# Delta rule of a hybrid layer: four heads' key norms in one go, one decay matrix per head through DRAM, six jobs at a time, and two chunk chains half a head apart

## The chip, the cores and the metric

The kernel runs on 1 core of one Trainium2 chip. The metric is the device time of one execution in microseconds (us). The core has a matrix engine (PE, with its weight loads shown apart as PEld), a vector engine (DVE), an activation engine (ACT), a general engine (POOL), and a queue engine (SP) that issues most of the DMA transfers. Each engine works through its own instructions in program order.

## The reference, cut to what matters

Two layers act on x (512 tokens, 2048 channels). The even layer is chunked attention plus an mLSTM; nothing of it changes. The odd layer projects to 6160 columns, runs an RG-LRU on eight blocks and a gated delta rule on eight heads, and projects back. The delta rule is what changes:

```python
    decay = jnp.cumsum(gc, axis=-1)
    gam = jnp.exp(jnp.where(tril, decay[..., :, None] - decay[..., None, :], NEG))
    kbeta = kc * bc[..., None]
    a_mat = jnp.where(strict, jnp.einsum('nbhtd,nbhsd->nbhts', kbeta, kc) * gam, 0.0)
    t_inv = lax.linalg.triangular_solve(eye + a_mat, ...)
    ...
    def step(st, inp):
        un, wn, qdn, qkn, kdn, dln = inp
        v_new = un - jnp.einsum('bhtk,bhkv->bhtv', wn, st)
        o = jnp.einsum('bhtk,bhkv->bhtv', qdn, st) + jnp.einsum('bhts,bhsv->bhtv', qkn, v_new)
        st = dln[..., None, None] * st + jnp.einsum('bhsk,bhsv->bhkv', kdn, v_new)
        return st, o
```

q and k are normalised to unit length first. The kernel uses chunks of 128 tokens, so a head has four of them.

## The kernel before

**Stream and jobs.** `run` walks over a list of units: four K-tiles of one weight tile each. A unit of the odd layer's input projection is 12 matmuls of 128x512 (lines 291 to 293: high half by high half, high by low, low by high of float32 values split in two). The weights of a unit come by DMA on SP, are split by an ACT copy (line 247) and a DVE subtraction (line 248), and this split is issued `AHEAD` = 5 units before the unit's matmuls. After every second K-tile, that is after six matmuls, `run` calls `tick`, and `tick` lets each active job (a Python generator) issue its next piece of instructions:

```python
    def tick(self):
        while len(self.active) < self.nact and self.jobs:
            self.active.append(self.jobs.popleft())
        for g in list(self.active):
            if next(g, self) is self:
                self.active.remove(g)
```

`yield from self.wait("name")` lets `LAG["name"]` ticks pass. So the order on every engine is fixed when the program is built; a LAG that is too short shows as a matmul in PE's queue whose input isn't there yet, and the weight stream waits behind it.

**The odd layer.** The stream brings the eight heads' k tiles, then x and gate tiles of LRU blocks 0 to 3, then q, v, z of heads 0 to 7, then LRU blocks 4 to 7 (48 weight tiles), and then the output projection, which reads the 16 tiles of `y1` (LRU 0 to 3, heads 0 to 7, LRU 4 to 7); its first four weight tiles run interleaved, four K-tiles of each in turn. The jobs stand in this order: `start1` (norm and gates), eight `delta_keys`, `solve`, four `lru_block`, then `inverse(h+1)` and `delta_head(h)` in turn, and four `lru_block`. Four jobs are active at a time until `solve` is done, and six from then on.

- `delta_keys(h)` (lines 1155 to 1196): convolution, SiLU, four transposes (1165), squares and their sum (1173); writes k and its transpose to DRAM (1162, 1174); then the inverse norm by 14 vector instructions on 128x4 values (1179, helper lines 623 to 629) and the columns derived from it (1181 to 1186); the decay matrix with the strict triangle by two POOL subtractions and one Exp (`gamma`, lines 1149 to 1152), times a column on POOL (1188); k by k on PE (1193); product on DVE (1194), written to DRAM as `ud`.
- `solve` (1198 to 1224): inverts the 32x32 diagonal blocks of all heads at once, 31 steps of one DVE product (1214) and one DVE sum (1220), both growing with n*n, each step followed by a wait of `1 + n * n // LAG['sv.n']` ticks.
- `inverse(h)` puts the blocks together to 128x128 inverses; it starts when `solve` is done and `self.heads >= h - 1`, and scales the transposed keys on POOL (1241).
- `delta_head(h)`: convolutions of q and v; the decay matrix a second time, now with the diagonal (POOL 1278, 1279, Exp 1282, times a column on POOL 1284); q by k (1291), transposes of v (1297); then, once the head before has finished (`while self.heads < h`), the chain over four chunks: state by keys (`dh.ks`, 1310, into DVE 1313), inverse by that (`dh.xr`, 1316, into DVE 1318), update of the state (`dh.kv`, 1322, into DVE 1325 or 1327). The output matmuls (1311, 1329) go between these steps. Then norm, gate and `put`.

Weight tiles' results are evicted by DVE with the row norms (`evict`, line 453; `evict_pad`, line 481). Scratch tiles come from small pools: `tmp` (6 buffers), `ev` (13), `act` slots (37), and 4 PSUM banks `pm` for the jobs.

Of the kernel before, what the change touches and what calls it, by code (L numbers as in the profile page):

```python
# [8 lines left out]
F32 = mybir.dt.float32  # L9
F32R = mybir.dt.float32r  # L10
# [6 lines left out]
P = 128  # L17
# [19 lines left out]
EPS = 1e-6  # L37
NEG = -1e30
# [10 lines left out]
Y1_ORDER = list(range(4)) + [8 + i for i in range(8)] + list(range(4, 8))  # L49
# [3 lines left out]
for _h in range(4):  # L53
# [15 lines left out]
    "conv": 2, "gam": 8, "sv": 8,  # L69
    "sv.n": 300,  # L70
# [5 lines left out]
    "dh.kq": 5, "dh.vt": 1, "dh.first": 4, "dh.ks": 1, "dh.xr": 2, "dh.kv": 2, "dh.ss": 4,  # L76
# [4 lines left out]
class Net:  # L81
# [9 lines left out]
    def __init__(self, ctx, tc, a):  # L91
# [32 lines left out]
        self.heads = self.turn = 0  # L124
# [608 lines left out]
    def start0(self, raw):  # L733
# [20 lines left out]
        self.tri1 = self.triangle(-NEG, -1)  # L754
# [260 lines left out]
    def layer1(self):  # L1015
# [4 lines left out]
        self.ud = self.dr.tile([8, P, S], F32, name="ud")  # L1020
        self.xd = self.dr.tile([P, 32, 32], F32, name="xd")
# [5 lines left out]
        for n in range(4):  # L1027
            add((n, "x"), self.evict_pad)
            add((n, "zc"), self.evict)
        for h in range(8):  # L1030
            add((h, "q"), self.evict_pad)
            add((h, "v"), self.evict_pad)
            add((h, "z"), self.evict)
        for n in range(4, 8):
            add((n, "x"), self.evict_pad)
            add((n, "zc"), self.evict)
# [3 lines left out]
        self.jobs += [self.delta_keys(h) for h in range(8)]  # L1040
        self.jobs += [self.solve()]
        self.jobs += [self.lru_block(n) for n in range(4)]
        self.jobs += [self.inverse(0)]
        for h in range(8):
            self.jobs += [self.inverse(h + 1)] if h < 7 else []
            self.jobs += [self.delta_head(h)]
        self.jobs += [self.lru_block(n) for n in range(4, 8)]
# [5 lines left out]
    def start1(self):  # L1053
# [8 lines left out]
        self.kcols = self.mp.tile([P, 8, 4, 4], F32, name="kcols")  # L1062
# [28 lines left out]
    def delta_gates(self, g):  # L1091
# [35 lines left out]
        nc.vector.tensor_scalar(self.ncols, self.cols[:, 1], -1.0, None, ALU.mult)  # L1127
        self.t["gates1"] = True
# [16 lines left out]
    def gamma(self, h, db, g, tri):  # L1145

        nc = self.nc
        yield
        nc.gpsimd.tensor_tensor(self.c4(g), self.c4(db), self.mask_bc(tri), ALU.subtract)
        nc.gpsimd.tensor_tensor(self.c4(g), self.c4(g), self.col_bc(self.cols[:, 0, :, h]), ALU.subtract)  # L1150
        yield from self.wait("gam")
        nc.scalar.activation(g, g, AF.Exp)
        yield

    def delta_keys(self, h):
# [10 lines left out]
        kt, g = self.ev(), self.ev()  # L1166
        sq = self.tmp()
        nc.scalar.activation(kt, ps, AF.Copy)
        ss = self.small(P, 4)
        nc.scalar.activation(sq, kt, AF.Square)  # L1170
        db = self.dec_bc(h)
        yield from self.wait(2)
        nc.vector.tensor_reduce(ss, self.c4(sq), AX.X, ALU.add)
        nc.gpsimd.dma_start(self.ktd[h], kt)
        while "gates1" not in self.t:
            yield

        nc.vector.tensor_scalar(ss, ss, 4 * EPS, None, ALU.add)
        r = self.rsqrt_cols(ss)
        kc = self.kcols[:, h]  # L1180
        nc.vector.tensor_copy(kc[:, 0], r)
        nc.vector.scalar_tensor_tensor(kc[:, 1], ss, 0.5, r, ALU.mult, ALU.mult)
        nc.vector.tensor_tensor(kc[:, 2], r, self.cols[:, 3, :, h], ALU.mult)
        nc.vector.tensor_tensor(kc[:, 3], r, self.cols[:, 2, :, h], ALU.mult)
        nb = self.small(P, 4)
        nc.vector.scalar_tensor_tensor(nb, kc[:, 2], -1.0, r, ALU.mult, ALU.mult)
        yield from self.gamma(h, db, g, self.tri1)
        nc.gpsimd.tensor_tensor(self.c4(g), self.c4(g), self.col_bc(nb), ALU.mult)
# [5 lines left out]
        nc.vector.tensor_tensor(g, g, ps, ALU.mult)  # L1194
        nc.gpsimd.dma_start(self.ud[h], g)
# [30 lines left out]
    def inverse(self, h):  # L1226

        nc = self.nc
        while "solved" not in self.t or self.heads < h - 1:
            yield  # L1230
# [10 lines left out]
        nc.gpsimd.tensor_tensor(self.c4(kd), self.c4(kd), self.col_bc(self.kcols[:, h, 3]), ALU.mult)  # L1241
# [24 lines left out]
    def delta_head(self, h):  # L1266
        nc, mp = self.nc, self.mp
        cs = lambda t, c: t[:, c * P : c * P + P]
        while self.heads < h - 1:
            yield  # L1270
# [4 lines left out]
        kc = self.kcols[:, h]  # L1275
# [5 lines left out]
        yield from self.wait("gam")  # L1281
# [17 lines left out]
        nc.vector.tensor_tensor(self.c4(vt), self.c4(ps), self.col_bc(kc[:, 1]), ALU.mult)  # L1299
# [4 lines left out]
        op = self.psum("dh.o")  # L1304
        st = None
        for c in range(4):
            rt = cs(vt, c)
# [187 lines left out]
```

## Time and profile before

| | |
|---|---|
| runs | 1854.64, 1988.14, 1854.49 us; median 1854.64 |
| profiled execution | 1853.82 us, its span 1852.0 us |
| busy PE / DVE / ACT / POOL | 1829.2 / 1340.3 / 877.9 / 217.5 us |
| mean granted TensorE clock | 0.998 |

The page gives busy time by engine, the span in 40 slices, the DMA queues, the chain that ended last, and groups of instructions. A busy PE isn't PE at its peak, since matmuls are pipelined and overlap: a row's duration is longer than the distance to the next one. So the distances between matmuls are read in the timeline, and the waits of PE in the view of waits. The layer that changes lies between about 1030 and 1720 us.

### The profile page before, as it was taken

How to read it: one execution, taken by the hardware profiler on the slowest of the kernel's cores; microseconds unless marked ns; L12 is line 12 of the kernel's file. 1: busy time of each engine (PE TensorE's matmuls, PEld its weight loads, DVE VectorE, ACT ScalarE, POOL GpSimd, SP SyncE). 2: the span in 40 equal slices, each digit the busy share in tenths (PEclk: the TensorE clock that was granted, in tenths of full speed). 3: DMA queues.
4: the chain of work that ended last, by engine and by line, in shares of the span. 5: the costliest groups of instructions: out<-in, count | busy, mean ns of one | idle time of the engine just before them, and what ended most of it. 6: DMA issues, size and time to landing. Idle time of an engine off the chain costs nothing.

```text
span 1852.0 us, 27588 instructions
## 1 busy us (share of the span) xinstructions
PE 1829.2 (99%) x10162; PEld 1566.2 (85%) x10162; DVE 1340.3 (72%) x2367; ACT 877.9 (47%) x1528; POOL 217.5 (12%) x262
## 2 busy tenths in 40 slices
PE   9999999999999999999999999999999999999999
PEld 7789899989889899988899788887788878787998
DVE  6768658798647368787766799889647667768664
ACT  6365445655435354665434553454333434566332
POOL 0010101110100101011111023301202122000000
PEclk9999999999999999999999999999999999999999
DMA  6243333333434343237554444433433433245542
GB/s 226 80 136 103 108 115 113 110 100 116 127 98 121 101 124 102 88 97 221 187 160 147 126 142 155 150 114 104 143 103 109 118 114 100 77 134 161 176 135 73
DMA packets 137288, 232.13 MB, mean 125 GB/s; under 512 B 22896, under 2 KB 32240, under 8 KB 137152
## 3 DMA queue, kind: packets, MB, share of 16 engines
q1 hardware_dynamic: 129488, 208.60, 37.0%
q0 software_dynamic: 5360, 17.57, 2.6%
q10 hardware_dynamic: 2304, 4.20, 0.6%
q8 instruction: 80, 1.31, 0.3%
q14 instruction: 56, 0.46, 0.1%
HBM read 203.79 MB, written 26.51 MB: 124 GB/s over the span
## 4 chain that ended last, share of the span: by engine, by line
PE 80%; DVE 12%; issue 3%; ACT 2%; DMA 2%; SPq 1%; DVEq 0%; ACTq 0%
PE pp L365 39%; PE pp L291 8%; PE pp L293 8%; PE pp L292 8%; PE pp L427 3%; PE pp L429 3%; PE pp L428 3%; DVE act L248 3%; DVE act L1214 1%; DMA act<-in_xT 1%; ACT act L247 1%; DVE act L1137 1%; DVE ev L1137 1%; DMA wr<-in_wi 0%; SPq L1207 0%
## 5 line engine op out<-in xcount | busy, mean ns | idle before, releaser
L365 PE MATMUL pp<-act,act 128*128 128x256 f32 (+1 forms) x4884 | 794.5, 322 | 0.0
L365 PEld LDWEIGHTS pp<-act,act 128*128 128x128 f32 x4884 | 707.0, 190 | 70.1
L248 DVE TENSOR_TENSOR act<-wr,act 128x512 fp32r<-128x512 f32 x719 | 507.7, 721 | 242.1 <-ACT act L247 239.6
L247 ACT ACTIVATE act<-wr 128x512 fp32r<-128x512 f32 x719 | 419.9, 622 | 188.6 <-DVE wr L222 61.0
L291 PE MATMUL pp<-act,act 128*128 128x512 f32 x960 | 389.4, 406 | 2.0 <-ACT act L563 1.3
L293 PE MATMUL pp<-act,act 128*128 128x512 f32 x960 | 377.0, 393 | 3.8 <-DVE act L248 3.7
L292 PE MATMUL pp<-act,act 128*128 128x512 f32 x960 | 376.0, 392 | 0.9 <-DVE act L564 0.8
L293 PEld LDWEIGHTS pp<-act,act 128*128 128x128 f32 x960 | 180.9, 188 | 45.0 <-DVE act L248 6.0
L291 PEld LDWEIGHTS pp<-act,act 128*128 128x128 f32 x960 | 181.5, 189 | 41.5 <-issue 3.8
L292 PEld LDWEIGHTS pp<-act,act 128*128 128x128 f32 x960 | 181.4, 189 | 36.5 <-DVE act L564 1.5
L427 PE MATMUL pp<-act,act 128*128 128x512 f32 x256 | 100.3, 392 | 0.0
L429 PE MATMUL pp<-act,act 128*128 128x512 f32 x256 | 99.7, 390 | 0.0
L428 PE MATMUL pp<-act,act 128*128 128x512 f32 x256 | 99.7, 389 | 0.0
L222 DVE TENSOR_TENSOR wr<-wr,wr 128x512 f32<-128x512 f32 x111 | 77.1, 695 | 1.3
L381 ACT ACTIVATE ee<-pp 128x512 f32<-128x512 f32 x74 | 44.1, 595 | 61.6 <-PE pp L365 61.3
L980 POOL TENSOR_SCALAR pq<-pq,mx 128x512 f32<-128x512 f32 (+3 forms) x32 | 47.3, 1491 | 188.7 <-DVE mx L977 188.7
L528 POOL DMA_DIRECT2D yd<-ev x20 | 11.4, 570 | 401.5 <-DVE ev L1011 163.9
L429 PEld LDWEIGHTS pp<-act,act 128*128 128x128 f32 x256 | 48.1, 188 | 10.1
L428 PEld LDWEIGHTS pp<-act,act 128*128 128x128 f32 x256 | 48.1, 188 | 9.7
L427 PEld LDWEIGHTS pp<-act,act 128*128 128x128 f32 x256 | 48.1, 188 | 9.6
L784 DVE TENSOR_TENSOR ev<-ev,pp 128x512 f32<-128x512 f32 x32 | 22.0, 688 | 46.9 <-PE pp L365 43.2
L593 ACT ACTIVATE act<-ev 128x512 fp32r<-128x512 f32 x40 | 25.0, 629 | 52.2 <-DVE ev L938 31.0
(334 smaller groups left out, 1992.0 us busy)
## 6 DMA issues: line engine op xcount, KB each, us to landing
wr<-in_wi SPq DMA_DIRECT2D x216, 256.0 KB
wr<-in_ws SPq DMA_DIRECT2D x100, 256.0 KB
wr<-in_wd SPq DMA_DIRECT2D x100, 256.0 KB
wr<-in_wv SPq DMA_DIRECT2D x64, 256.0 KB
wr<-in_wso SPq DMA_DIRECT2D x48, 256.0 KB
wr<-in_wdo SPq DMA_DIRECT2D x48, 256.0 KB
wr<-in_wo SPq DMA_DIRECT2D x32, 256.0 KB
ev<-x1d SPq DMA_DIRECT2D x28, 256.0 KB
```

Source lines behind the costliest of these rows:

```text
L222: sub = lambda o, x, y: nc.vector.tensor_tensor(o, x, y, ALU.subtract)
L247: nc.scalar.activation(h, w, AF.Copy)
L248: nc.vector.tensor_tensor(l, w, h.bitcast(F32), ALU.subtract)
L291: nc.tensor.matmul(ps, h[:, j, :], xh, start=k == 0, stop=False)
L292: nc.tensor.matmul(ps, h[:, j, :], xl, start=False, stop=False)
L293: nc.tensor.matmul(ps, l[:, j, :], xh, start=False, stop=k == KT - 1)
L365: mm = lambda o, x, y, start=False: nc.tensor.matmul(o, x, y, start=start, stop=True, skip_group_check=True)
L381: nc.scalar.activation(e, ps, AF.Copy)
L427: nc.tensor.matmul(ps, xh, h, start=k == 0, stop=False)
L428: nc.tensor.matmul(ps, xh, l, start=False, stop=False)
L429: nc.tensor.matmul(ps, xl, h, start=False, stop=k == KT - 1)
L980: nc.gpsimd.tensor_scalar(rows(b), rows(b), mx[:, 3, b : b + 1], None, ALU.mult)
```

## The change

- `delta_keys` is cut in three. `keys(h)` goes as far as the sum of squares. `key_norms(h0)` computes the norms of four heads at once, on 128x16 values. `couplings(h)` reads k back from DRAM, builds the decay matrix once (with the diagonal) by one POOL subtraction and four Exps with the decay as a bias column, writes it to DRAM (`gd`), and multiplies k by k with it and with a column in four DVE instructions.
- `delta_head` reads `gd` instead of building the decay matrix; norms no longer scale it, and the column of `vn` takes their square instead. `inverse` scales the transposed keys by four ACT copies instead of one POOL product.
- The heads' turn is counted in chunks (`self.blocks`): a head's chain starts when the chain before it has done two of four chunks, and `inverse` and `delta_head` start half a head earlier too. The steps' waits are longer (`dh.ks` 1 to 2 ticks, `dh.xr` 2 to 3, `dh.kv` 2 to 3). The seven output matmuls of a head stand together at its end.
- Six jobs are active from the start of the layer, and `solve` waits longer (`sv.n` 300 to 220). `lru_block` takes its gate weights' buffers from the common pools. The order of the stream is the same, written in another way.

```diff
+RS = 12
-    "conv": 2, "gam": 8, "sv": 8,
-    "sv.n": 300,
+    "conv": 2, "gam": 5, "dk.db": 3, "dh.q": 6, "sv": 8,
+    "sv.n": 220,
-    "dh.kq": 5, "dh.vt": 1, "dh.first": 4, "dh.ks": 1, "dh.xr": 2, "dh.kv": 2, "dh.ss": 4,
+    "dh.kq": 5, "dh.vt": 1, "dh.first": 4, "dh.ks": 2, "dh.xr": 3, "dh.kv": 3, "dh.ss": 4,
...
-        self.jobs += [self.delta_keys(h) for h in range(8)]
+        self.jobs += [self.keys(h) for h in range(4)] + [self.key_norms(0)]
+        self.jobs += [f(h + 4 * i) for h in range(4) for i, f in ((1, self.keys), (0, self.couplings))]
+        self.jobs += [self.key_norms(4)] + [self.couplings(h) for h in range(4, 8)]
         self.jobs += [self.solve()]
...
-        self.nact = 4
+        self.nact = 6
...
+    def key_norms(self, h0):
+
+        nc = self.nc
+        yield from self.take(*((h, "ss") for h in range(h0, h0 + 4)))
+        while "gates1" not in self.t:
+            yield
+        half, b, nb = [self.kcols[:, i, h0 : h0 + 4] for i in range(3)]
+        flat = half.rearrange("p h c -> p (h c)")
+        nc.vector.tensor_scalar(flat, flat, 4 * EPS, None, ALU.add)
+        r = self.rsqrt_cols(flat).rearrange("p (h c) -> p h c", c=4)
+        nc.vector.tensor_tensor(b, r, r, ALU.mult)
+        nc.vector.scalar_tensor_tensor(half, half, 0.5, r, ALU.mult, ALU.mult)
+        nc.vector.tensor_tensor(b, b, self.cols[:, 3, :, h0 : h0 + 4].rearrange("p c h -> p h c"), ALU.mult)
+        nc.vector.tensor_scalar(nb, b, -1.0, None, ALU.mult)
+        for h in range(h0, h0 + 4):
+            self.t[h, "norms"] = True
+
+    def couplings(self, h):
+
+        nc = self.nc
+        yield from self.take((h, "norms"))
+        db, k, g = self.dec_bc(h), self.ev(), self.ev()
+        nc.sync.dma_start(k, self.kfd[h])
+        yield from self.wait("dk.db")
+        nc.gpsimd.tensor_tensor(self.c4(db), self.c4(db), self.mask_bc(self.tri), ALU.subtract)
+        yield from self.wait("gam")
+        for c in range(4):
+            nc.scalar.activation(self.c4(g)[:, c], self.c4(db)[:, c], AF.Exp, bias=self.ndec[:, c, h : h + 1])
+        nc.gpsimd.dma_start(self.gd[h], g)
+        yield from self.wait("dk.kk")
+        ps = self.psum("dk.kk")
+        u = db
         for c in range(4):
             kc = k[:, c * P : c * P + P]
             nc.tensor.matmul(ps[:, c * P : c * P + P], kc, kc, start=True, stop=True)
+        for c in range(4):
+            nc.vector.scalar_tensor_tensor(self.c4(u)[:, c], self.c4(ps)[:, c], self.kcols[:, 2, h, c : c + 1], self.c4(g)[:, c], ALU.mult, ALU.mult)
+        nc.gpsimd.dma_start(self.ud[h], u)
...
     def inverse(self, h):
-        while "solved" not in self.t or self.heads < h - 1:
+        while "solved" not in self.t or self.blocks < 4 * h - 6:
...
-        nc.gpsimd.tensor_tensor(self.c4(kd), self.c4(kd), self.col_bc(self.kcols[:, h, 3]), ALU.mult)
+        for c in range(4):
+            nc.scalar.activation(self.c4(kd)[:, c], self.c4(kd)[:, c], AF.Copy, scale=self.cols[:, 2, c, h : h + 1])
...
     def delta_head(self, h):
-        while self.heads < h - 1:
+        while self.blocks < 4 * h - 6:
...
+        nc.sync.dma_start(att, self.gd[h])
-        nc.gpsimd.tensor_tensor(self.c4(att), self.c4(db), self.mask_bc(self.tri), ALU.subtract)
-        nc.gpsimd.tensor_tensor(self.c4(att), self.c4(att), self.col_bc(self.cols[:, 0, :, h]), ALU.subtract)
-        yield from self.wait("gam")
-        nc.scalar.activation(att, att, AF.Exp)
+        yield from self.wait("dh.q")
-        nc.gpsimd.tensor_tensor(self.c4(att), self.c4(att), self.col_bc(kc[:, 0]), ALU.mult)
...
-        while self.heads < h:
+        while self.blocks < 4 * h - 2:
...
-                nc.tensor.matmul(cs(op, c), st, cs(q, c), start=True, stop=False)
...
-            nc.tensor.matmul(cs(op, c), vn, cs(att, c), start=not c, stop=True)
...
+        op = self.psum("dh.o")
+        for c in range(4):
+            if c:
+                nc.tensor.matmul(cs(op, c), st[c], cs(q, c), start=True, stop=False)
+            nc.tensor.matmul(cs(op, c), vn[c], cs(att, c), start=not c, stop=True)
```

## Rows read from the trace of the kernel before

**Rows 1.** The page: span, and PE's busy time and share.
```profile
span 1852.0 us, 27588 instructions
...
PE 1829.2 (99%) x10162; PEld 1566.2 (85%) x10162; DVE 1340.3 (72%) x2367; ACT 877.9 (47%) x1528; POOL 217.5 (12%) x262
```

**Rows 2.** Timeline of PE, first and last of 43 matmuls: start, us, what.
```profile
1126.37 0.40 PE L292 MATMUL pp<-act,act 128*128 128x512 f32 x1
...
1135.90 0.39 PE L292 MATMUL pp<-act,act 128*128 128x512 f32 x1
```

**Rows 3.** Waits of PE, 1030 to 1740 us: us in total, times, longest.
```profile
PE pp L293 <- DVE act L248: 3.7, 2, 2.2
PE dh_vt L1297 <- DVE act L672: 2.4, 1, 2.4
PE dk_tr L1165 <- DVE ev L672: 1.3, 1, 1.3
...
PE dh_kv L1322 <- issue: 1.2, 1, 1.2
...
PE dh_ks L1310 <- DVE r L1325: 0.6, 1, 0.6
```

**Rows 4.** Stretches: PE, PEld, DVE, ACT, POOL busy, granted clock, DMA share, GB/s.
```profile
1090.00:1140.00 50.00, 50.00 (x240) 41.77 (x239) 47.48 (x123) 19.52 (x35) 17.81 (x24) 1.00 0.46 153
...
1240.00:1300.00 60.00, 53.98 (x232) 43.63 (x231) 58.10 (x74) 21.89 (x36) 11.27 (x13) 0.96 0.41 121
1300.00:1350.00 50.00, 50.00 (x304) 40.89 (x304) 29.48 (x51) 15.10 (x29) 7.29 (x9) 0.98 0.42 126
```

**Rows 5.** Timeline of PE, two neighbours of the slow spell behind a wait.
```profile
1282.61 0.63 PE L291 MATMUL pp<-act,act 128*128 128x512 f32 x1
1283.03 0.63 PE L292 MATMUL pp<-act,act 128*128 128x512 f32 x1
```

**Rows 6.** DVE by line, 1240 to 1302 us: busy us, mean ns | idle before.
```profile
L1214 DVE TENSOR_TENSOR act<-act,act 128x256 f32<-128x256 f32 (+15 forms) x16 | 19.6, 1227 | 0.0
L248 DVE TENSOR_TENSOR act<-wr,act 128x512 fp32r<-128x512 f32 x21 | 17.3, 839 | 1.1 <-ACT act L247 1.1
...
L1220 DVE TENSOR_REDUCE act<-act 128x16 f32<-128x256 f32 (+15 forms) x16 | 12.0, 750 | 0.6
```

**Rows 7.** DVE by line, 1090 to 1200 us.
```profile
L626 DVE TENSOR_TENSOR sm<-sm 128x4 f32<-128x4 f32 x24 | 6.3, 262 | 0.8
...
L1194 DVE TENSOR_TENSOR ev<-ev,dk_kk 128x512 f32<-128x512 f32 x8 | 5.5, 682 | 0.7 <-PE dk_kk L1193 0.7
...
L1184 DVE TENSOR_TENSOR kcols<-sm,dcols 128x4 f32<-128x4 f32 x8 | 1.2, 156 | 0.0
```

**Rows 8.** The page's costliest groups: the split over the whole span.
```profile
L248 DVE TENSOR_TENSOR act<-wr,act 128x512 fp32r<-128x512 f32 x719 | 507.7, 721 | 242.1 <-ACT act L247 239.6
```

**Rows 9.** DVE by line and shape, 1030 to 1740 us: a chain step.
```profile
L1313 DVE SCALAR_TENSOR_TENSOR r<-dh_ks,ncols,act 128x128 f32<-128x128 f32 x24 | 8.3, 347 | 13.9 <-PE dh_ks L1310 13.9
```

**Rows 10.** Line 855: ns min/median/max, first and last start, form.
```profile
L855 ACT ACTIVATE pk<-tmp,ccol x16: 387/389/406, 125.7 to 748.3; 128x128 f32<-128x128 f32 x16
```

**Rows 11.** POOL by line and shape, 1030 to 1740 us.
```profile
L1278 POOL TENSOR_TENSOR act<-tmp,tri 128x512 f32<-128x512 f32 x8 | 12.4, 1548 | 12.3 <-PE pp L293 12.3
...
L1284 POOL TENSOR_TENSOR act<-act,kcols 128x512 f32<-128x512 f32 x8 | 8.9, 1112 | 11.4 <-ACT act L1282 11.3
```

**Rows 12.** DMA issues: count, KB each, median us to landing.
```profile
kfd<-ev POOLq DMA_DIRECT2D x8, 256.0 KB, 4.6
```

**Rows 13.** Timeline of PE: one chain step of head 0 and the next chunk's.
```profile
1345.88 0.38 PE L1310 MATMUL dh_ks<-r,act 128*128 128x128 f32 x2
...
1353.88 0.38 PE L1310 MATMUL dh_ks<-r,act 128*128 128x128 f32 x2
```

**Rows 14.** Line 1343 (last product of a head) and 453 (evictions): first, last start.
```profile
L1343 DVE TENSOR_TENSOR act<-act,ev x8: 691/691/693, 1391.8 to 1675.9; 128x512 f32<-128x512 f32 x8
...
L453 DVE TENSOR_TENSOR ev<-pp,rb x40: 410/425/693, 65.3 to 1680.0; 128x256 f32<-128x256 f32 x22, 128x512 f32<-128x512 f32 x18
```

More of the change, by code (lines that the diff above doesn't have):

```diff
@@ L48 @@
 Y0_ORDER = [t for i in range(4) for t in (8 + 2 * i, 9 + 2 * i, 2 * i, 2 * i + 1)]
-Y1_ORDER = list(range(4)) + [8 + i for i in range(8)] + list(range(4, 8))
+Y1_TILES = "l0 l1 l2 l3 h0 h1 h2 h3 h4 h5 h6 h7 l4 l5 l6 l7".split()
+Y1_ORDER = [int(t[1]) + 8 * (t[0] == "h") for t in Y1_TILES]
+STREAM1 = "l0 l1 l2 l3 h0 h1 h2 h3 h4 h5 h6 h7 l4 l5 l6 l7".split()
 FIRST0 = [(0, n) for n in ("k0", "k1", "q0", "q1")] + [(1, "k0"), (1, "k1")]
@@ L123, in __init__ @@
         self.spilt = {}
-        self.heads = self.turn = 0
+        self.blocks = self.turn = 0
         self.paired = {"x0", "y0", "y1"}
@@ L1026, in layer1 @@
             add((h, "k"), self.evict_pad)
[L1027 to L1036, printed above, removed]
+        for t in STREAM1:
+            n = int(t[1])
+            for name, f in (("x", self.evict_pad), ("zc", self.evict)) if t[0] == "l" else (("q", self.evict_pad), ("v", self.evict_pad), ("z", self.evict)):
+                add((n, name), f)
         self.tiles(specs[:3], 3)
@@ L1039, in layer1 @@
         self.jobs += [self.start1()]
-        self.jobs += [self.delta_keys(h) for h in range(8)]
+        self.jobs += [self.keys(h) for h in range(4)] + [self.key_norms(0)]
+        self.jobs += [f(h + 4 * i) for h in range(4) for i, f in ((1, self.keys), (0, self.couplings))]
+        self.jobs += [self.key_norms(4)] + [self.couplings(h) for h in range(4, 8)]
         self.jobs += [self.solve()]
[L1042 to L1047, printed above, removed]
+        for t in STREAM1:
+            n = int(t[1])
+            if t[0] == "l":
+                self.jobs += [self.lru_block(n)]
+            else:
+                self.jobs += [self.inverse(0)] if n == 0 else []
+                self.jobs += [self.inverse(n + 1)] if n < 7 else []
+                self.jobs += [self.delta_head(n)]
         self.jobs += [self.all_sums("y1")]
@@ L1143, in dec_bc, with keys @@
         return t
[L1145 to L1150, printed above, removed]
-        yield from self.wait("gam")
-        nc.scalar.activation(g, g, AF.Exp)
-        yield
-    def delta_keys(self, h):
+    def keys(self, h):
         nc = self.nc
@@ L1309, in delta_head @@
                 ps = self.psum("dh.ks")
-                nc.tensor.matmul(ps[:, :P], cs(kf, c), st, start=True, stop=True)
-                nc.tensor.matmul(cs(op, c), st, cs(q, c), start=True, stop=False)
-                rt = self.small(P, P, "r", 6)
+                nc.tensor.matmul(ps[:, :P], cs(kf, c), st[c], start=True, stop=True)
+                rt = self.small(P, P, "r", RS)
                 nc.vector.scalar_tensor_tensor(rt, ps[:, :P], self.ncols[:, c, h : h + 1], cs(vt, c), ALU.mult, ALU.add)
@@ L1348, in lru_block @@
         cv = yield from self.take((n, "x"))
-        gw = self.mp.tile([P, 256], F32, tag="gw", name=self.uid("gw"), bufs=1)
-        gp = [self.mp.tile([P, 256], F32R, tag=t, name=self.uid(t), bufs=1) for t in ("gh", "gl")]
+        gw, gp = self.tmp()[:, :256], self.slot(F32R)
+        gp = [gp[:, i, :256] for i in range(2)]
         nc.sync.dma_start(gw, self.a["gw"][n])
@@ L1450, in host @@
     cols = [kd + P * h for h in range(8)]
-    for n in range(4):
-        cols += [xc + P * n, zc + P * n]
-    for h in range(8):
-        cols += [qd + P * h, vd + P * h, zd + P * h]
-    for n in range(4, 8):
-        cols += [xc + P * n, zc + P * n]
+    for t in STREAM1:
+        cols += [b + P * int(t[1]) for b in ((xc, zc) if t[0] == "l" else (qd, vd, zd))]
     d["wi1"] = tiles(w1, cols)
```

54 lines of the change are left out of this document (19 added, 35 removed).

## The prediction

> **What bounds the kernel now.** The page first: PE is busy for 1829.2 of 1852.0 us [rows 1], which looks as if nothing could be had. But a matmul's row lasts 0.39 us, and 43 of them in the weight stream start from 1126.37 to 1135.90, that is 42 distances of 0.227 us [rows 2]. So busy time hides the first 0.16 us of each wait, and the stream's own pace is 0.227 us a matmul. All of PE's work stays in the changed kernel: the same transposes, products and chain steps, in other places. A gain can then come only from waits of PE and from time at a lower clock, and a loss only from new waits. The view of PE's waits over the layer has nine rows [rows 3]: 3.7 us on the weight split (line 248) and 2.4 us on a SiLU of head 0, both on DVE; 1.3 us on a key's SiLU; four rows of chain steps, from 1.2 down to 0.6 us, 3.3 us together; and two rows at the output projection that the change doesn't reach.
>
> The stretches say where. From 1240 to 1300 us DVE is busy for 58.1 of 60 us and PE for only 53.98 [rows 4]: here DVE is the bound, since `solve` (lines 1214, 1220) has its largest steps and the weight split stands behind them in DVE's queue. The granted clock averages 0.96 there and 0.98 in the next 50 us [rows 4]; in such a spell neighbours start 0.42 us apart instead of 0.227 [rows 5], the lower of the clock's two levels (1.2 instead of 2.4 GHz), right behind waits of PE. From 1090 to 1140 us DVE is busy for 47.48 of 50 us as well, yet PE never idles [rows 4]: a split is issued five units ahead of its use, and a unit is 12 matmuls, so DVE may be late by 5 x 12 x 0.227 = 13.6 us before PE waits (an estimate from the distance and from `AHEAD`).
>
> **What can be had.** The stretch of `solve`: 3.7 + 2.4 = 6.1 us of waits [rows 3], three of them, each hiding another 0.16 us: 0.5; and the clock: 0.04 x 60 + 0.02 x 50 = 3.4 us [rows 4]. Together 10.0 us. The key's SiLU: 1.3 + 0.16 = 1.5 us. The chain steps: 3.3 us in six waits, with what they hide 4.3 us. In all 15.8 us.
>
> **Part 1, `sv.n` 300 to 220.** The waits between the 31 steps are 1 + n*n//300 ticks, 54 in all; with 220 they are 67. The 16 largest steps (n = 16 to 31), which are those of [rows 6], took 39 ticks and will take 51. A tick is six matmuls, 1.36 us, so the stream gives them 53 us now and 69 us then. DVE's demand: 19.6 + 12.0 = 31.6 us for these steps [rows 6], a split per two ticks (19.5 now, 25.5 then) at 0.721 us [rows 8], 14.1 or 18.4 us, and about 9 us of other work (58.1 less 31.6 and 17.3), 9 or 12 us. That is 54.7 us in 53 us now, over the bound and made worse by the slower splits of [rows 6], 0.839 us; and 62 us in 69 us then. With six jobs, though, head 1's convolutions can fall into the same stretch: six instructions and two SiLUs of about 0.86 us or less, 6.5 us more, 68.5 of 69. So most of the stall goes, not surely all: I take 8 of 10.0 us, bounds 0 and 10. `solve` itself ends little later: 13 ticks more are 18 us, less 10 us of stall; what stands behind it is `inverse(0)` and the heads.
>
> What the row shows of POOL in this: the split takes 0.839 us where POOL works 11.27 of 60 us [rows 4, 6] and 0.721 us over the whole span [rows 8], 21 x 0.118 = 2.5 us. The Trainium skill's GPSIMD Engine Reference, section Key points, says that POOL shares its SBUF interfaces with the vector engine and contends with DVE instructions that have two SBUF inputs; the split is one, and this trace agrees in sign. By the rule, with six of seven POOL products gone, these 2.5 us would come off DVE's demand and the stall would go wholly; by the sum above, which doesn't count on it, 2 us of it stay.
>
> **Part 2, norms of four heads at once.** Twelve groups of 128x4 instructions, from 6.3 us (line 626) to 1.2 us (line 1184), take 39.2 us of DVE between 1090 and 1200 us [rows 7]. Two rounds of 20 instructions on 128x16 replace eight; by the same rows 39.2/8 = 4.9 us a round, 10 us. DVE is freed of some 29 us there. The path doesn't see it, as PE idles there only once: the wait of 1.5 us on the key's SiLU, which stands behind such a round. I take that 1.5 us as gained, bounds 0 and 1.5.
>
> **Part 3, `couplings`.** The product on DVE was one instruction of 0.682 us a head [rows 7]; four of 128x128 out of PSUM with a column replace it, nearest row 0.347 us [rows 9], 1.4 us a head, 5.6 us more in all. The four Exps with a bias column have their row in the even layer, 0.389 us [rows 10]: four a head and 32 in all, since the matrix is built once, 12.4 us; with 32 copies for the transposed keys at about the same price another 12.4 us, against 16 whole Exps that go. ACT is busy for 19.5 of 50 us there [rows 4] and hides that. New is the burst: heads 4 to 7 get their norms in one tick, so their four `couplings` run in step: 16 Exps (6.2 us on ACT) in one tick, later 16 products (5.6 us on DVE) and all four matmul groups in another, with four PSUM banks for them. 5.6 us is under DVE's 13.6 us, and PE could wait for a bank only for one product. I take 1 us lost, bounds 0 and 5.6.
>
> POOL loses six of the seven groups of 8 products between 12.4 and 8.9 us [rows 11], 53 to 74 us; that is idle time of an engine that isn't the bound. It gets eight more DMA issues, behind which stand the small memsets of `evict_pad`; it waited for the same Exp before. SP gets 16 more reads and POOL eight more writes of 256 KB, 6.3 MB, at a DMA share of 0.46 [rows 4]. A read of k waits for its write, 4.6 us to land [rows 12], issued two to three ticks (2.7 to 4.1 us) before: SP stands up to 2 us, and behind it stand weight loads, which run ahead by more than the split does. Cost nothing; without that cover 2 us four times.
>
> **Part 4, the chains.** A chunk took 1353.88 - 1345.88 = 8.0 us [rows 13] in 5 ticks (6.8 us); with 8 ticks it takes 8 x 1.36 + 1.2 = 12.1 us, a head 48 instead of 32 us. But a head starts 24 us after the one before instead of 32 and four ticks. So the heads don't fall back against the stream, which brings one per three weight tiles, 24 ticks. Each step has one tick more for its DVE instruction of 0.347 us [rows 9], and with two chains a tick can hold two steps, one behind the other. I take 3 of 4.3 us, bounds 0 and 4.3. What is late next: the last head's product starts at 1675.9, while the stream's last eviction is at 1680.0 [rows 14]; the projection reads heads 4 to 7 only in its third group of units, 2 x 4 x 12 x 0.227 = 22 us on. So heads may come 26 us later before PE waits.
>
> **Sum.** 1853.82 us of the profiled execution, 1852.0 of them span, less 8, 1.5 and 3, plus 1: 1842.3 us. The median of the runs is 0.8 us higher; I predict 1842.
>
> **Rivals.**
> - *The stall stays.* Head 1's work comes fully into the stretch and DVE stays over its bound, with the clock falling as before. For it: 68.5 of 69 us. Against: 29 us less DVE work just ahead. With none of the 10 us: 1853.8 - 4.5 + 1 = 1850; if the chains gain nothing either, and for this trace the change does nothing, 1854.
> - *Slower: buffers.* Up to three heads are in flight (a head enters when the one two before is half done) with three `act` slots each instead of two heads, beside 16 of x and some seven of weights out of 37, and four `couplings` hold four of six `tmp` and eight of 13 `ev`. A split or an eviction then waits for a slot that a chain still reads. It decides once such waits pass 13.6 us: then each head costs PE its excess. At 2 us a head 1842 + 16 = 1858; at 6 us 1890. Against: no row shows a wait of PE for a slot now.
> - *More than forecast.* All 15.8 us and no loss: 1838, and with it the relief of 2.5 us on DVE at POOL's side (the rule above).
>
> **How the numbers follow.** The forecast, 1839 to 1847, 0.55; the stall stays, 1848 to 1855, 0.22; slower by buffers or bursts, 1856 and up, 0.15, of which 0.03 above 2%; more than forecast, below 1839, 0.08. Bounds: all gains and no loss give 1838, and 5.6 us lost with no gain 1859. The range that holds 8 in 10 runs from 1836 to 1858; the forecast's own is 1839 to 1847. Within 2% (37 us, about what a measurement of this kernel can tell from no change) lies nearly all of it: faster than that would need more than twice the 15.8 us there are, 0.01; slower 0.03; the same 0.96.
>
> **What would show it.** Right: from 1240 to 1300 us DVE under 95% and the granted clock 1.00, the split gone from PE's waits or under 1.5 us; the twelve groups of norms at about 10 us; chain rows in PE's waits under 1.5 us; chunk steps 12 us apart. Wrong: PE's waits on line 248 or on a PSUM bank near 1190 us, or ACT and DVE waiting for slots between 1350 and 1650 us; or a wait behind the heads' last tiles after 1700 us.

## The result

The changed kernel takes 1841.41 us (median of four runs, 1840.04 to 1842.42) beside 1854.57 us before: a ratio of 0.9937, 95% interval 0.9925 to 0.9949, so some 12 us less (the medians lie 13.2 us apart, the spans 11.4). One of the four runs before, of 1988.14 us, is a slow one and left out of the ratio. The profiled execution took 1842.42 us, its span is 1840.6 us, to be set against that of [rows 1].

The page: span, then busy time of each engine.

```profile
span 1840.6 us, 27587 instructions
...
PE 1825.8 (99%) x10162; PEld 1568.1 (85%) x10162; DVE 1298.5 (71%) x2270; ACT 888.2 (48%) x1576; POOL 162.8 (9%) x220
```

DVE lost 41.8 us and POOL 54.7 us against [rows 1]; PE does the same 10162 matmuls. All waits of PE from 1030 to 1740 us (us in total, times, longest), which answer to [rows 3]:

```profile
PE dh_vt L1308 <- DVE act L677: 1.9, 1, 1.9
PE pp L296 <- ACT act L568: 1.3, 1, 1.3
PE dh_kq L1302 <- DVE act L677: 1.0, 1, 1.0
PE dh_ks L1320 <- DVE r L1334: 0.6, 2, 0.4
PE pp L297 <- DVE act L569: 0.3, 1, 0.3
```

The weight split (now line 253) and the key's SiLU are gone from the list. Of `solve`'s stretch two waits on SiLUs of the first heads are left, and of the chains one row of 0.6 us. The stretches that answer to [rows 4], with the end of the heads and the tail (PE, PEld, DVE, ACT, POOL busy, granted clock, DMA share, GB/s):

```profile
1090.00:1140.00 50.00, 50.00 (x242) 41.82 (x241) 38.33 (x79) 24.95 (x50) 12.93 (x22) 1.00 0.63 197
1140.00:1200.00 60.00, 60.00 (x290) 50.45 (x289) 42.55 (x85) 28.05 (x57) 17.39 (x25) 1.00 0.58 187
...
1240.00:1300.00 60.00, 57.11 (x257) 46.61 (x256) 56.99 (x73) 21.33 (x35) 3.63 (x10) 1.00 0.42 132
1300.00:1350.00 50.00, 50.00 (x306) 40.98 (x305) 26.66 (x49) 17.41 (x37) 1.94 (x5) 1.00 0.54 157
...
1550.00:1650.00 100.00, 99.58 (x526) 82.87 (x525) 67.42 (x120) 55.83 (x90) 5.71 (x11) 1.00 0.36 109
1650.00:1722.00 72.00, 70.36 (x337) 59.00 (x336) 58.78 (x97) 43.39 (x71) 0.00 (x0) 0.98 0.58 183
```

From 1240 to 1300 us PE is busy for 57.11 us instead of 53.98, and the clock is 1.00 instead of 0.96, and 1.00 instead of 0.98 behind it: 3.1 + 3.4 us, and 0.2 us for one hidden part less, 6.7 us. The key's SiLU gives the 1.5 us. From 1350 to 1650 us PE idles for 0.6 us; before, it idled for 3.6 us there (0.10, 1.01 and 2.48 in three stretches of 100 us). So the chains give 3.0 us, about 3.4 with what busy time hides (an estimate). The tail of the kernel before, to be set against the last row above,

```profile
1650.00:1722.00 72.00, 69.91 (x306) 56.92 (x305) 57.57 (x96) 45.08 (x70) 0.53 (x2) 1.00 0.56 179
```

idled for 2.1 us at full clock; now it is 1.6 us at 0.98: 1.4 us of clock less 0.5, some 1 us given back. Sum: 6.7 + 1.5 + 3.4 - 1.0 = 10.6 of 11.4 us. The rest lies ahead of the layer or in rounding.

### The profile page after: what moved, and what is told of

Its sections match the earlier page's. It is cut to its first block, busy times and chain, and to the rows that moved or that the text cites. A ratio compares the mean times of both kernels' runs of the same rounds, so it can differ in the third digit from the quotient of the medians.

```text
span 1840.6 us, 27587 instructions
## 1 busy us (share of the span) xinstructions
PE 1825.8 (99%) x10162; PEld 1568.1 (85%) x10162; DVE 1298.5 (71%) x2270; ACT 888.2 (48%) x1576; POOL 162.8 (9%) x220
## 4 chain that ended last, share of the span: by engine, by line
PE 86%; DVE 8%; ACT 2%; issue 2%; DMA 1%; SPq 1%; DVEq 0%; ACTq 0%; POOLq 0%
PE pp L370 39%; PE pp L296 9%; PE pp L298 9%; PE pp L297 9%; PE pp L432 3%; PE pp L434 3%; PE pp L433 3%; DVE act L253 2%; DVE act L1228 1%; ACT act L252 1%; SPq L1221 0%; PE inv_z L1265 0%; PE gates L418 0%; PE at_tr L999 0%; PE inv_t L1272 0%
## 5 line engine op out<-in xcount | busy, mean ns | idle before, releaser
L253 DVE TENSOR_TENSOR act<-wr,act 128x512 fp32r<-128x512 f32 x719 | 502.0, 713 | 264.0 <-ACT act L252 261.6
L533 POOL DMA_DIRECT2D yd<-ev x20 | 11.3, 565 | 406.4 <-DVE ev L1015 164.5
```

The source lines that it names most:

```text
L253: nc.vector.tensor_tensor(l, w, h.bitcast(F32), ALU.subtract)
```

## The experiments

The runs stand on several chips, so kernels are compared by the ratio to the kernel before on the same chip; 0.001 is 1.85 us. The difference of two ratios is uncertain by about 0.0018, 3.3 us (two half-widths of 0.0012 to 0.0013 in quadrature). So +1.1, +2.8 and, at the border, +3.3 aren't told apart from no change.

| what | median, us | ratio, 95% interval | against after (before), us |
|---|---|---|---|
| after, `sv.n` 300 | 1848.06 | 0.9967, 0.9954 to 0.9980 | +5.6 |
| before, `sv.n` 220 | 1852.51 | 0.9989, 0.9979 to 0.9998 | (-2.0) |
| after, norms head by head | 1857.47 | 1.0019, 1.0010 to 1.0028 | +15.2 |
| after, couplings 8 ticks later | 1847.33 | 0.9967, 0.9955 to 0.9978 | +5.6 |
| after, three more POOL products a head | 1856.30 | 1.0015, 1.0006 to 1.0024 | +14.5 |
| before, six groups of POOL products out | 1847.37 | 0.9968, 0.9956 to 0.9981 | (-5.9) |
| the same, `sv.n` 220 | 1847.26 | 0.9967, 0.9954 to 0.9980 | (-6.1) |
| after, short chain steps | 1848.11 | 0.9972, 0.9960 to 0.9983 | +6.5 |
| after, short steps, one chain at a time | 1845.77 | 0.9955, 0.9941 to 0.9970 | +3.3 |
| after, four jobs | 1855.65 | 1.0010, 1.0001 to 1.0019 | +13.5 |
| after, `dh.kq` 8, `dh.vt` 3 | 1842.87 | 0.9943, 0.9929 to 0.9958 | +1.1 |
| the same, operands two units earlier | 1844.59 | 0.9952, 0.9937 to 0.9967 | +2.8 |

### `solve`'s waits, undone and alone

```diff
-    "sv.n": 220,
+    "sv.n": 300,
```

> The changed kernel with the wait between the steps of the block inversion put back (sv.n 220 to 300), all else changed. Theory A (the spread of the 31 steps over 67 instead of 54 ticks is what took the stall out of the stretch from 1240 to 1300 us): PE waits on the weight split or on head 0's SiLU there again for 6 us or so, with a spell at the lower clock, and 6 to 9 us of the 13 us are given back: 1847 to 1850 us. Theory B (the stall went because the norms and POOL's products left DVE free ahead of and in this stretch): at most 2 us are lost, 1841 to 1844 us, and no wait on the split comes back.

Theory A in time: some 5.6 us of the gain go. PE's waits there are 2.5 us on an LRU block's operand (line 607, not foreseen), 1.9 us on a SiLU, as in the changed kernel, and 1.8 us on the split. From 1240 to 1300 us:

```profile
1240.00:1300.00 60.00, 54.00 (x233) 43.72 (x234) 57.63 (x74) 25.46 (x46) 3.62 (x10) 0.97 0.50 146
```

That is nearly the row of the kernel before [rows 4], with POOL at 3.6 instead of 11.3 us: the lighter POOL and norms alone don't lift this stall. The other way round, 220 in the kernel before:

```diff
-    "sv.n": 300,
+    "sv.n": 220,
```

> The kernel before with nothing changed but the divisor of solve's waits, 300 to 220. Theory A (the prediction's part 1 stands by itself: DVE is over its bound only while solve's largest steps run, and longer waits relieve it whatever the keys' part does): the row of the weight split (line 248) goes from PE's waits, DVE is under 95% from 1240 to 1300 us, and the time falls by 6 to 9 us, to about 1845 to 1848 us beside 1853.6. Theory B (the divisor is worth something only together with the lighter keys' part, since DVE comes into solve late by what the norms cost it, and with the other work that six active jobs bring in earlier): at most 3 us, 1850 to 1853, and a wait on a split or a SiLU stays behind solve. A divisor of 300 in the changed kernel gave up 5.6 us, so the two parts would add if this run gains 6 us or so.

The difference of the medians is 1.1 us, by the ratio 2.0 (0.4 to 3.9). Yet the stall is gone: PE is busy for 59.32 us at full clock. What it gives is lost elsewhere:

```profile
1240.00:1300.00 60.00, 59.32 (x268) 48.96 (x268) 59.27 (x77) 23.97 (x40) 7.76 (x12) 1.00 0.42 129
...
1550.00:1650.00 100.00, 93.13 (x513) 75.28 (x512) 70.43 (x121) 53.19 (x87) 12.33 (x15) 0.97 0.32 95
```

PE's waits name chain steps, 7.1 us in four waits. Six stream matmuls stand right ahead of the longest, which ends at 1603.78 us, as in any tick; it is DVE that was late. The waits, and DVE's timeline ahead of that one (start, us, what):

```profile
PE dh_ks L1310 <- DVE r L1325: 4.6, 2, 3.0
PE dh_ks L1310 <- DVE r L1327: 2.5, 2, 2.2
```

```profile
1598.10 1.22 DVE L1378 TENSOR_TENSOR_SCAN ev<-act,ev 128x512 f32<-128x512 f32 x1
1599.24 2.30 DVE L1137 SCALAR_TENSOR_TENSOR ev<-cv,cst,ev 128x512 f32<-128x512 f32 x3
...
1602.78 0.69 DVE L1343 TENSOR_TENSOR act<-act,ev 128x512 f32<-128x512 f32 x1
1603.38 0.34 DVE L1325 SCALAR_TENSOR_TENSOR r<-r,act,dh_kv 128x128 f32<-128x128 f32 x1
```

The chain's 0.34 us stand behind a scan and three convolution steps of LRU blocks and a head's last product; `dh.ks` = 1 tick doesn't cover that. The last sum of `solve` starts 6.9 us later than before (1303.9 for 1297.0) and the last head's product 15.6 us later (1691.5 for 1675.9 [rows 14]), so the last chains meet other jobs' bursts than before. So neither theory as worded holds: the divisor does lift the stall by itself, and most of what it gives is given back 300 us on, at steps that the changed kernel has made longer.

### The norms, and the ticks they bring

Norms head by head on 128x4 values, two ticks between heads, all four flagged at the end:

```diff
-        half, b, nb = [self.kcols[:, i, h0 : h0 + 4] for i in range(3)]
...
+        for h in range(h0, h0 + 4):
+            half, b, nb = [self.kcols[:, i, h] for i in range(3)]
...
+            yield from self.wait(2)
```

> The changed kernel with the norms made head by head on 128x4 values again (two ticks between heads), so that DVE has its some 29 us of small instructions back between 1090 and 1200 us; the couplings of four heads still start together. Theory A (DVE's load there is hidden behind the split's lead): 0 to 2 us lost, 1841 to 1843.5 us, with the two rounds taking 39 us of DVE instead of about 10. Theory B (the freed DVE time is what took the stall out of the later stretch): 5 us or more lost, 1846 us and up, with waits of PE on the split between 1240 and 1300 us.

It lost 15 us. That lies in theory B's open range, but not by its mechanism: the waits on the split come to 0.5 us, and the largest wait of PE stands at 1139 us on a key's SiLU. DVE's rows ahead of it, and POOL's in the same time:

```profile
PE dk_tr L1161 <- DVE ev L677: 5.1, 1, 5.1
```

```profile
1131.43 0.17 DVE L628 TENSOR_SCALAR sm<-kcols 128x4 int32<-128x4 int32 x1
1131.63 4.12 DVE L629 TENSOR_SCALAR sm<-sm 128x4 int32<-128x4 int32 x1
```

```profile
1131.36 0.54 POOL L1168 DMA_DIRECT2D ktd<-ev  x1 [16.88 <-ACT ev L1164]
1131.92 3.77 POOL L1196 TENSOR_TENSOR tmp<-tmp,tri 128x512 f32<-128x512 f32 x3
```

An instruction on four values a partition, of a kind that lasts 0.17 us, lasted 4.12 us and ended when POOL's three subtractions did; it started in the DMA issue of POOL right ahead of them. But the edit also delays the couplings by eight ticks a round. Those alone, with the norms left as changed:

```diff
         nc.vector.tensor_scalar(nb, b, -1.0, None, ALU.mult)
+        yield from self.wait(8)
```

> The changed kernel with the norms of four heads at once as they are, but eight ticks (48 matmuls, 10.9 us) between them and the couplings that wait for them, in both rounds. The run with norms head by head lost 15 to 17 us; it had the same eight ticks and some 60 more DVE instructions a round. Theory A (the loss there was not DVE's load, but that everything behind the norms is issued 8 ticks later and meets other work: solve, inverse(0) and the first heads come late for what reads them): most of the loss comes back here, 1852 to 1858 us. Theory B (the loss was DVE's load and its collision with POOL's runs in that stretch, not the ticks): at most 3 us slower than the changed kernel, 1840 to 1844 us, and no wait of PE on DVE between 1090 and 1200 us.

5.6 us, between the two theories. Its waits are those at the heads: 3.5 us on the result of line 1328 (1327 in the changed kernel), 1.9 on `dh.ks`, 2.5 instead of 1.3 at the tail; none lies between 1090 and 1200 us. So of the 15 us some 10 (an estimate, 15.2 less 5.6; the parts needn't add) are DVE's load and POOL's hold, and the rest may be a mere shift.

### POOL's products

```diff
         nc.scalar.activation(ed, db, AF.Exp)
+        for _ in range(3):
+            nc.gpsimd.tensor_tensor(self.c4(db), self.c4(db), self.mask_bc(self.tri), ALU.subtract)
```

> The changed kernel with three more POOL subtractions of 128x512 per head in delta_head, right behind the Exp that reads the decay rows; they act on a scratch tile that nothing reads afterwards, so that only POOL's load changes (24 instructions of about 1.2 us, near what the kernel before had there: two subtractions and a product). Theory A (the prediction: POOL's products are idle time of an engine that isn't the bound): at most 1 us slower, 1841 to 1843 us. Theory B (POOL's runs hold DVE instructions off, as in the run with norms head by head, where one DVE instruction on 128x4 values lasted 4.12 us while POOL ran three subtractions): DVE instructions beside these runs last longer by about one run each, the chain steps and the SiLUs of q and v come later, PE's waits on them grow by 0.2 to 0.7 us a head, and the time is 2 to 6 us longer, 1844 to 1848 us.

Theory B, but far beyond its range: 14.5 us, more than the whole gain, for work that nobody waits for (in the trace no instruction waits for these 24). The page's busy times, PE's largest wait, and the timelines of POOL and DVE around one of the runs:

```profile
PE 1832.0 (99%) x10162; PEld 1570.0 (85%) x10162; DVE 1317.6 (71%) x2270; ACT 888.5 (48%) x1576; POOL 199.2 (11%) x244
```

```profile
PE dh_ks L1322 <- DVE r L1336: 6.3, 4, 2.7
```

```profile
1409.40 4.83 POOL L1294 TENSOR_TENSOR tmp<-tmp,tri 128x512 f32<-128x512 f32 x3 [9.99 <-ACT act L1292]
```

```profile
1409.59 5.19 DVE L1142 SCALAR_TENSOR_TENSOR act<-cv,cst,act 128x512 f32<-128x512 f32 x3
1416.41 2.32 DVE L1142 SCALAR_TENSOR_TENSOR act<-cv,cst,act 128x512 f32<-128x512 f32 x3
```

Three convolution steps take 2.32 us with POOL quiet and 5.19 us beside its run. POOL is held as well: its 24 subtractions last from 1.29 to 2.13 us, median 1.62. DVE has the same 2270 instructions and is busy for 19.1 us more, for 36.4 us more of POOL: 0.52 us for each. Then the opposite, in the kernel before:

```diff
-        nc.gpsimd.tensor_tensor(self.c4(g), self.c4(db), self.mask_bc(tri), ALU.subtract)
-        nc.gpsimd.tensor_tensor(self.c4(g), self.c4(g), self.col_bc(self.cols[:, 0, :, h]), ALU.subtract)
...
-        nc.scalar.activation(g, g, AF.Exp)
+        nc.scalar.activation(g, db, AF.Exp, bias=self.bias_col(-30.0))
...
-        nc.gpsimd.tensor_tensor(self.c4(g), self.c4(g), self.col_bc(nb), ALU.mult)
```

and the same three products in `delta_head`.

> The kernel before without six of its seven groups of POOL products (lines 1149, 1150, 1188, 1278, 1279, 1284: 48 instructions, 60 us of POOL); the two Exps read the decay rows instead, shifted by a constant, so the masks, the decay differences and the scaling by the norms are left out of what is computed. DVE keeps every instruction, the norms head by head too, and no wait is changed. Theory A (the prediction: what POOL loses is idle time of an engine that isn't the bound, beyond 2.5 us of DVE at the splits): 1850 to 1853 us beside 1853.6. Theory B (POOL's runs hold DVE off wherever both work, as three more subtractions per head did in the changed kernel, at 15 us): DVE's rows of 0.84 to 0.90 us in the layer go to 0.68 to 0.77, DVE is under 95% from 1240 to 1300 us, and most of the change's gain comes by this alone, 1843 to 1848 us.

5.9 us (3.5 to 8.2) faster: theory B in time, with half of the change's gain, but not in its sign, since DVE stays at 58.10 of 60 us from 1240 to 1300 where B had it under 95%:

```profile
PE 1827.6 (99%) x10162; PEld 1568.0 (85%) x10162; DVE 1308.9 (71%) x2368; ACT 877.9 (48%) x1528; POOL 158.3 (9%) x214
```

```profile
1240.00:1300.00 60.00, 55.43 (x242) 44.99 (x241) 58.10 (x75) 21.96 (x36) 8.17 (x11) 0.97 0.43 128
```

DVE has one instruction more than before (a constant) and is busy for 31.4 us less, for 59.2 us less of POOL: 0.53 for each, the same price as the other way. The key's SiLU is out of PE's waits without any change to the norms. But PE is busy for 55.43 of 60 us in `solve`'s stretch, only 1.5 us better than before: one of the two waits on the split is left. POOL still works for 8.17 us there; with the run with 300 above, which has 3.6 us and the stall whole, it shows that this stall isn't POOL's in the main. With both edits:

> The same without the six groups of POOL products (left out of what is computed), and with the divisor of solve's waits at 220. The divisor alone gave the kernel before 1.1 us (0.2 to 2.1). Theory A (POOL's load costs nothing): the sum of the two, 1849 to 1852 us. Theory B (the longer waits of solve can only pay once DVE isn't held off and late): more than the two single gains together, at the changed kernel's time or below, 1839 to 1844 us; PE is busy for 59 us or more of 1240 to 1300.

The time of the one edit, neither theory. `solve`'s stretch is clean (first row, PE 60.00), and the last chains give it back again:

```profile
1240.00:1300.00 60.00, 60.00 (x272) 49.80 (x271) 59.28 (x80) 24.39 (x40) 5.96 (x13) 1.00 0.47 143
...
1550.00:1650.00 100.00, 93.16 (x520) 75.71 (x519) 68.31 (x121) 50.39 (x82) 7.78 (x13) 0.98 0.34 106
```

```profile
PE dh_ks L1304 <- DVE r L1319: 4.6, 2, 3.0
```

The waits of 4.6 us are those of the run with 220 alone, where POOL worked too, to the tenth: these come from the order of DVE's work, not from POOL.

### The chains

```diff
-    "dh.kq": 5, "dh.vt": 1, "dh.first": 4, "dh.ks": 2, "dh.xr": 3, "dh.kv": 3, "dh.ss": 4,
+    "dh.kq": 5, "dh.vt": 1, "dh.first": 4, "dh.ks": 1, "dh.xr": 2, "dh.kv": 2, "dh.ss": 4,
```

> The changed kernel with the short steps of the chain (dh.ks 1, dh.xr 2, dh.kv 2 ticks), two chains still half a head apart. Theory A (longer steps took the chain's waits away): PE's waits on chain steps come back, some 2 to 4 us, 1843 to 1846 us. Theory B (the steps were never late enough to matter, or the gain there came from fewer DVE and POOL instructions in the heads): within 1 us of the changed kernel, 1840 to 1842.5 us.

More than either: 6.5 us. And with `while self.blocks < 4 * h:` ahead of the chain besides, so that one runs behind the other:

> The changed kernel with the short steps and the chains one behind the other again, as before the change; matmuls of the output stay together at the end. Theory A (the chains' order only matters through late steps): as with short steps alone, 2 to 4 us lost, 1843 to 1846 us, the heads ending some 15 to 25 us later under the cover of the stream. Theory B (chains half a head apart are worth something by themselves): more than 4 us lost, 1846 us and up, with waits behind the last heads at the output projection.

3.3 us, as theory A had it. PE's waits of the first and of the second:

```profile
PE dh_ks L1320 <- DVE r L1334: 3.4, 4, 1.7
PE dh_ks L1320 <- DVE r L1336: 3.2, 5, 1.1
```

```profile
PE dh_ks L1320 <- DVE r L1336: 2.4, 1, 2.4
...
PE dh_ks L1320 <- DVE r L1334: 1.3, 2, 1.0
```

Short steps cost waits in either order, with two chains more often; the 3 us between the two runs are within their uncertainty. Long steps with one chain at a time weren't tried, so the overlap's own worth stays open.

### Six jobs

```diff
-        self.nact = 6
+        self.nact = 4
```

(at the layer's start; six from `solve`'s end on, as before.)

> The changed kernel with four active jobs instead of six until solve is done. Theory A (six jobs only bring other work forward, and the heads have 26 us to spare): within 1.5 us of the changed kernel, 1840 to 1843 us. Theory B (with two jobs less the couplings and the first LRU blocks come later, solve ends later, and inverse(0) and head 0 with it): 3 us or more slower, 1845 to 1850 us, with PE's waits on SiLUs and chains behind solve. The opposite is possible too: less DVE work from LRU blocks and convolutions beside solve, so that the wait of 1.9 us on a SiLU at line 1308 goes, 1838 to 1840 us.

Theory B, and beyond its range: 13.5 us. PE's first waits and `solve`'s stretch:

```profile
PE pp L298 <- DVE act L253: 3.7, 3, 2.1
PE dh_vt L1308 <- DVE act L677: 3.6, 1, 3.6
```

```profile
1090.00:1140.00 50.00, 50.00 (x236) 41.64 (x234) 35.41 (x70) 20.61 (x41) 8.60 (x16) 1.00 0.56 181
1140.00:1200.00 60.00, 60.00 (x296) 50.52 (x295) 38.65 (x79) 24.11 (x55) 18.39 (x30) 1.00 0.59 199
...
1240.00:1300.00 60.00, 51.40 (x226) 41.20 (x225) 57.40 (x79) 23.85 (x40) 5.08 (x13) 0.98 0.40 124
1300.00:1350.00 50.00, 50.00 (x283) 40.88 (x283) 32.10 (x50) 13.23 (x28) 1.34 (x2) 0.95 0.45 140
```

DVE does 6.8 us less from 1090 to 1200 us, where it has room, and 5.4 us more from 1300 to 1350. So six jobs draw work forward, and `solve` with it: its first step is at 1203.5 us with six and at 1213.6 with four. But they don't draw work out of its 16 largest steps: while these run, DVE does 18.1 us of other work than the steps and the splits with six jobs and 15.6 with four. How six jobs keep this stretch clear isn't shown. The bare shift of eight ticks above, which has the last sum of `solve` as late (1309.6 us) as four jobs have it (1308.5, against 1297.3), cost 5.6 us alone; so not all of the 13.5 need be the jobs' doing.

### What was left

```diff
-    "dh.kq": 5, "dh.vt": 1, "dh.first": 4,
+    "dh.kq": 8, "dh.vt": 3, "dh.first": 4,
```

> The changed kernel with longer waits ahead of two products that PE still waits for: dh.kq 5 to 8 ticks and dh.vt 1 to 3. PE's waits of the changed kernel on the SiLU of line 677 are 1.9 us (transposes of v, line 1308) and 1.0 us (q by k, line 1302), both in head 0 and 1. Theory A (what is left of waits in the changed kernel can be had in the same way, by more ticks): both rows go, 2.9 us with 0.3 us that busy time hides, 1838 to 1839.5 us. Theory B (five ticks more put each head's chain later, and what is gained comes back as waits on chain steps or on the inverse, line 1331 or 1316): 1840 to 1845 us, with new rows at the chains' lines.

Theory B by the waits; the time can't be told from the changed kernel's. From 1240 to 1300 us PE is busy for all 60 us, the waits of 1.9 and 1.0 us are gone, and others stand at the last chains:

```profile
1240.00:1300.00 60.00, 60.00 (x271) 49.45 (x270) 56.99 (x74) 23.00 (x39) 5.37 (x11) 1.00 0.44 138
```

```profile
PE dh_kv L1331 <- DVE r L1327: 1.9, 2, 1.2
```

And for the tail, `BACK` 5 to 7 and `LEAD` 3 to 5 besides:

> The run with dh.kq 8 and dh.vt 3 ticks, and beside that the operands of the stream split two units earlier (LEAD 3 to 5, and the reads of spilled tiles that feed them, BACK 5 to 7). That run kept PE's waits of 1.8 and 0.3 us on an operand's split (lines 568, 569) at 1686 us, with matmuls at the lower clock behind them (mean clock 0.98 from 1650 to 1722, 1.4 us). Theory A (the operand was ready earlier and only its split stood late in ACT's queue): the rows on 568 and 569 go and the clock stays up, 3 to 3.7 us faster than that run, 1838 to 1840 us. Theory B (the operand itself comes late from its LRU block, so an earlier place in the program changes nothing there, and splits issued earlier hold slots longer): no change or 1 to 3 us slower, 1842 to 1846 us.

Nearer to theory B: the row on line 568 is there still, and at 3.3 instead of 1.8 us. An earlier place in the program doesn't help, so the operand itself seems to be late; what makes it late wasn't followed further. No kernel tried is faster than the changed one.

## Why the prediction was right

The time came out as forecast, 1841.4 for 1842, and so did most of what the profile was to show. (The sum's 1842.3 is for the profiled execution, which took 1842.42; with the 0.8 us that it adds for the median it would have been 1843.) Not all of its steps held.

- **What bounds it, and what can be had.** Right: what was gained and can be placed is waits of PE and clock. The chain steps' 3.3 us are five waits, not six, so 4.1 us with what they hide and 15.6 in all.
- **Part 1.** Right in place, 6.7 us for 8, and in its working: while the 16 largest steps run, 69.5 us, DVE is busy for 66.2, with 18.1 us of other work, for 68.5 of 69 and 18.5 forecast. The splits went from PE's waits; two waits on the first heads' SiLUs stayed (1.9 and 1.0 us for the 2.4 of [rows 3]). DVE is at 56.99 of 60 us, 95%, the border named; but that was no good sign to go by, as the kernel before with 220 ran nearly without the stall at 59.27. The step on what is late next failed: heads 26 us later were to cost nothing, but with 220 in the kernel before the heads came 15.6 us later, and most of the gain was lost at chain steps that were still short. The bound looked at the heads' last tiles only, not at what a shifted step meets in DVE's queue. The changed kernel escapes this: `solve` starts 12.9 us earlier than before and ends at the same time (last sum at 1297.3 for 1297.0 us), which the prediction didn't count. And "six jobs" stood in the sum as a burden on this stretch; with four, PE idles there for 8.6 us instead of 2.9.
- **Part 2.** The norms take 7.6 us (rows below, 38 instructions) for 10 forecast and 39.2 before [rows 7]. A third of the 39.2 was POOL's hold: in the kernel before without six of its groups the same twelve groups take 26.5 us. The SiLU's 1.5 us came, but that run, with its norms head by head, has them too, so they needn't be the norms' doing. And "the path doesn't see it" was too short: with norms head by head the changed order loses some 10 us (the estimate above).
- **Part 3.** The burst costs nothing (PE 60.00 from 1140 to 1200), for 1 us forecast. **POOL at nothing is the step that failed.** Taking it away is worth 5.9 us by itself, and putting two thirds of it back costs 14.5. The prediction weighed 2.5 us, at the splits alone, and left them out of its sum; over the kernel DVE is freed of 31.4 us by it.
- **The rule weighed there.** The reading under it was wrong: the mean of 0.839 us isn't that of the splits that PE waited for. Of the 21 splits of [rows 6], 16 take some 0.68 us, two take 0.96 and 0.93 us, and three take 4.66 us together, beside POOL's products but behind PE's last wait on a split, which ends at 1280.5 us (row below). So some 0.5 us of hold stood ahead of these waits, not 2.5, and with POOL's products out most of the stall stayed: 55.43 of 60 us. In sign, DVE's rows agree with the Trainium skill's GPSIMD Engine Reference (Key points). The Trainium skill's page SBUF — State Buffer, section Who interferes with whom, says more: the shared ports go to one instruction for its whole length and the other waits, not at half speed. The runs agree that it is no mere slowing: 5.19 us for 2.32, and 4.12 for 0.17; but those 4.12 us span three products of POOL, not one. By the same section an instruction with one SBUF input takes part only in a two-port mode; whether the one of 4.12 us, which has one, ran in such a mode, no run here shows. By this rule all of POOL's 53 to 74 us would have wanted a price.
- **Part 4.** About 3.4 us for 3; `dh.ks` comes 11.7 us apart for 12.1 (below), the chain row is 0.6 us. With short steps it loses 3.3 or 6.5 us; why more than 3.4 isn't shown.
- **Not foreseen:** 1 us at the tail (line 568, and the spell behind it).

The three late splits before, on DVE's timeline; DVE by line, 1090 to 1200 us: the first and the last of the norms' eleven groups (six lines of the helper, five of `key_norms`; busy, mean ns); and PE's timeline at two chunks of head 0:

```profile
1298.72 4.66 DVE L248 TENSOR_TENSOR act<-wr,act 128x512 fp32r<-128x512 f32 x3
```

```profile
L1185 DVE TENSOR_SCALAR kcols<-kcols 128x16 f32<-128x16 f32 x2 | 1.4, 704 | 0.1
...
L1183 DVE SCALAR_TENSOR_TENSOR kcols<-kcols,sm 128x16 f32<-128x16 f32 x2 | 0.3, 168 | 0.0
```

```profile
1348.96 0.38 PE L1320 MATMUL dh_ks<-r,act 128*128 128x128 f32 x2
...
1360.66 0.38 PE L1320 MATMUL dh_ks<-r,act 128*128 128x128 f32 x2
```

So the sum was right partly by luck. Errors of its terms (burst, tail, `solve`) cancel. And part 1's gain, which the kernel before gives back with short steps, with or without POOL's products, stands here with longer steps, less work on POOL and an earlier `solve`. The sum counted the steps for the chains alone and the other two at nothing; which of the three part 1 needs isn't shown, as the kernel before with 220 and long steps wasn't tried. Undone singly, the parts lose 5.6, 15.2, 6.5 and 13.5 us, far more than the 12 us they bring together. They aren't additive, and a pure shift of eight ticks cost 5.6 us, so of any of these figures some 5 us may be shift, not cause; that one part protects the gain of another fits the runs, but isn't shown apart from that.

## What to carry to other kernels

Where one engine is nearly full in a stretch, ask of each relief not only whether the stall goes, but which step, moved later, meets which burst in that engine's queue; a gain was given back 300 us downstream three times here. Price work on POOL by what it holds up on DVE (here 0.5 us for each us), even where nobody waits for its result. And when each part undone loses more than all parts gain, measure a bare shift of the order before a cause is read into the loss.

## What the hardware showed unexpectedly

A small instruction of DVE can be held for as long as POOL works, and it isn't always: one `TENSOR_SCALAR` on 128x4 values lasted 4.12 us beside 3.77 us of subtractions, and in the changed kernel one on 128x16 values 1.23 us beside a run of four, about as long as one of these:

```profile
1167.97 1.23 DVE L1185 TENSOR_SCALAR kcols<-kcols 128x16 f32<-128x16 f32 x1
```

```profile
1167.88 6.48 POOL L1196 TENSOR_TENSOR tmp<-tmp,tri 128x512 f32<-128x512 f32 x4 [5.19 <-DMA tmp<-rows]
```

Over whole kernels the price was 19.1/36.4 = 0.52 and 31.4/59.2 = 0.53 us of DVE for each us of POOL's busy time, in which the time that POOL itself is held is counted. And the lower clock doesn't follow from a wait alone: PE's wait of 1.3 us on the operand's split stood in both kernels, at full clock before (1.00 from 1650 to 1722 us) and with a spell of matmuls 0.43 us apart behind it after (0.98):

```profile
1686.51 0.50 PE L296 MATMUL pp<-act,act 128*128 128x512 f32 x1 [1.34 <-ACT act L568]
...
1688.61 0.63 PE L298 MATMUL pp<-act,act 128*128 128x512 f32 x1
1689.04 0.63 PE L296 MATMUL pp<-act,act 128*128 128x512 f32 x1
```
